# Dilated attention: queries and keys stored by residue, the scores of two heads issued in turn, weights read along the queries

## The chip, the cores and the metric

The kernel runs on one NeuronCore of a Trainium2 chip. A core has five engines with a queue each: TensorE (PE in the profile, with its weight loads listed apart as PEld), VectorE (DVE), ScalarE (ACT), GpSimd (POOL) and SyncE (SP, which only starts DMAs here). Matmuls read SBUF and write PSUM, which has 8 banks of 128 partitions by 512 floats. The metric is the time of one execution on the device in microseconds (us): 1367.67 us, the median of three runs before (1365.44 to 1367.97).

## The reference

A trunk of two layers over 512 tokens of width 1024, all in float32. Each layer is a mixer and a gated feed-forward, each between two normalizations with modulation. Layer 0's mixer is a pool and a gated recurrence; layer 1's is the dilated attention, the only part that the change touches:

```python
DIL_GROUPS = ((128, 1), (512, 4), (2048, 16))   # window, dilation; 8 heads of width 64 in each
def dilated_group_attention(q, k, v, win, dil, bias_table):
    blk = win // dil                              # 128 in all three groups
    qs = _to_strided(q * 64 ** -0.5, dil, blk)    # tokens regrouped by residue modulo dil
    kk, vv = with_prev(ks), with_prev(vs)         # a block sees itself and the one before it
    ...
    s = einsum(qs, kk) + bias;  s = where(mask, s, -inf)
    m = max(s);  p = exp(s - m);  l = sum(p)
    o = einsum(p, vv) / l
# the three groups are joined per head: o = sum(l * exp(m - max) * o) / sum(l * exp(m - max))
```

With 512 tokens, group 0 has four blocks of 128 (each query sees its own block and the one before), group 1 has four residues modulo 4 with one block of 128 tokens each, and group 2 (16 residues) is computed on the same four residues with a mask that leaves the tokens of the same residue modulo 16.

## The kernel before

The work is staged in time: mixer 0, feed-forward 0, attention (about 664 to 975 us of the profile), feed-forward 1. Activations lie feature by token. Weight matmuls use a split into two parts (`hi`, `lo`) and three products; they all go through the helper `mm`, so the profile puts them on L263. The attention's own score matmuls are plain float32 and stand on their own lines.

The order on each engine is found by a scheduler that replays the program with its own times when the program is built (`schedule_with_timeline_sim=True`). It may move an instruction ahead of another that it doesn't depend on; PSUM banks, though, are handed out where the code asks for them, from a queue: `bk.get()` takes the bank that was given back longest ago, `bk.free()` puts it at the end.

The function `attention` (L1220) runs as follows.

- The head (L1225 to L1237): the queries (even `i`, scaled by 0.125, on ACT, L1231) and keys (odd `i`, on DVE, L1233) of the first pair of heads are copied from PSUM into SBUF, `i` = 0 to 5 being q0, k0, q1, k1, q2, k2 of the three groups. A tile holds two heads, head `hh` on partitions 64*hh to 64*hh+63, with the 512 tokens along the row.
- `values` makes V for the three groups (L1273).
- Then four pairs of heads. For pairs 1 to 3, six projections of 24 matmuls each (L1289) with copies on ACT and DVE (L1293, L1295). For every residue `r` of 0 to 3 and each of the two heads: 7 score matmuls (L1320 to L1326) into one bank; a reduction on DVE that adds the bias and takes the maximum (L1333), which frees the bank; the exponential with its sum on ACT (L1338); reciprocal and scaling on DVE (L1340, L1341); four transposes on PE into a second bank (L1344); a copy of that bank to `PT` on ACT (L1346).
- `weighted` (L1352) multiplies `PT` by V: group 0 in four steps over key blocks with the queries of all residues at once (L1368 to L1370), groups 1 and 2 residue by residue (L1372).
- With pair 3, four of the eight banks are set aside for the output projection (L1300), `weighted` runs in two halves of the tokens, and the output projection's first matmuls may fill PE between the scores.

Of the 7 score matmuls of a head, five have weights of 64 rows by 32 columns: `far` (L1320, a constant that masks a block which doesn't exist) and group 0's quarter `j` = 0 (L1321) both stand in column group 0, quarters 1 to 3 (L1323) in column groups 1 to 3. The two others (L1326, groups 1 and 2) have weights of 64 rows by 128 columns. Head 0 uses rows 0 to 63 of the array and head 1 rows 64 to 127 (`tile_position`). The operands for residue `r` are read with a step of four floats: `qv[ps, j, :, r]`, `z.rearrange("p (i r) -> p r i")`-like views `[ps, :, r]` of q1, k1, q2, k2. Only k0 is read in the order of the tokens.

Of the kernel before, what the change touches and what calls it, by code (L numbers as in the profile page):

```python
# [15 lines left out]
AF = mybir.ActivationFunctionType  # L16
ALU = mybir.AluOpType

P = 128
# [3 lines left out]
HT = T // 2  # L23
# [157 lines left out]
def trunk(ctx: ExitStack, tc: tile.TileContext, a: dict, out: bass.AP, last: int = 3):  # L181
    nc = tc.nc
    pe, act, dve, pool, sp = nc.tensor, nc.scalar, nc.vector, nc.gpsimd, nc.sync
# [8 lines left out]
    ar, rr, tr = Arena(), Arena(), Arena()  # L192
# [8 lines left out]
    def swing_to(*arenas):  # L201

        first = next((i for i in range(2) if swings[i]["of"] is not arenas[i]), 2)
        for z in reversed(swings[first:]):
            if z["of"] is not None:
                for i in range(len(z["units"])):
                    z["of"].drop(f"{z['name']}{i}")
                z["pool"].__exit__(None, None, None)
            z["of"] = None
        for z, arena in list(zip(swings, arenas))[first:]:  # L210
            if arena is None:
                continue
            n_swing[0] += 1
            z["of"], z["pool"] = arena, tc.tile_pool(name=f"swing{n_swing[0]}", bufs=1, reuse_waits="tile")
            p = z["pool"].__enter__()
            for i, u in enumerate(z["units"]):
                name = f"{z['name']}{i}"
                t = p.tile([P, u * UNIT], F32 if arena is ar else F32R, tag=name, name=f"swing{n_swing[0]}_{i}")
                arena.add(name, t, u)
# [277 lines left out]
    b = bk.get()  # L497
# [401 lines left out]
    for h in range(4):  # L899
        b = banks8[4 + h]  # L900
# [319 lines left out]
    def attention(s, chain):  # L1220
        ahead.update(load=N_QK, split=N_QK - 1, f=8, r=0)
        head_banks = project_head(s, w_qk, N_QK, chain)
        rr.closed.discard("o")
        swing_to(ar, ar)
        head_rs = []  # L1225
        for i in range(N_QK):
            r = ar.get(1)
            for hf in range(2):
                o, y = ar.ap(r)[:, hf * HT : (hf + 1) * HT], bk[head_banks[hf][i // 2]][:, (i % 2) * HT : (i % 2 + 1) * HT]
                if i % 2 == 0:  # L1230
                    act.activation(o, y, AF.Copy, scale=0.125)  # L1231
                else:
                    dve.tensor_copy(o, y)  # L1233
            head_rs.append(r)
        for z in head_banks:
            for b in z:
# [40 lines left out]
        for pair in range(4):  # L1277
            qk_rs = []
            pt_rs = [ar.get(4) for _ in range(2)]
            for x in (pair, pair + 1):  # L1280
                if x < 4 and x not in biases_of:
                    load_biases(x)
            bias_r, bias_t = biases_of[pair]
            for i in range(6):
                if pair * 6 + i < N_QK:
                    qk_rs.append(head_rs[i])
                    continue
                b = bk.get()
                project(w_qk2 + pair * 6 + i - N_QK, b)  # L1289
                ada_step(44)  # L1290
                r = ar.get(1)
                if i % 2 == 0:
                    act.activation(ar.ap(r), bk[b], AF.Copy, scale=0.125)  # L1293
                else:
                    dve.tensor_copy(ar.ap(r), bk[b])  # L1295
                bk.free(b)
                qk_rs.append(r)
            if pair == 3:
                ahead.update(load=14, split=4, f=2, r=0)
                out_banks = [bk.get() for _ in range(4)]  # L1300
                rr.add("h", h_t, 2 * ND)
                rr.used["h"] = [k % ND < 4 for k in range(2 * ND)]
                for _ in range(2):
                    split_next(0, pool)
                for i, r in enumerate(o_rs):
                    split_into(h_hi[:, i, :], h_lo[:, i, :], ar.ap(r))
                    ar.free(r)
            q0, k0, q1, k1, q2, k2 = (ar.ap(r) for r in qk_rs)
            PT = [ar.ap(r).rearrange("p (r s q) -> p r s q", r=4, s=4) for r in pt_rs]
            for r in range(4):  # L1310
                for hh in range(2):
                    head = 2 * pair + hh
                    ps = slice(64 * hh, 64 * hh + 64)
                    b = bk.get()
                    qv = q0.rearrange("p (j i r) -> p j i r", j=4, r=4)
                    for j in range(4):
                        js = slice(32 * j, 32 * j + 32)
                        kw = dict(start=True, stop=True, tile_position=(64 * hh, 32 * j), skip_group_check=True)
                        if j == 0:
                            pe.matmul(bk[b][js, 0:P], far[ps, :], one_row[ps, :], **kw)  # L1320
                            pe.matmul(bk[b][js, P : 2 * P], qv[ps, j, :, r], k0[ps, 0:P], **kw)  # L1321
                        else:
                            pe.matmul(bk[b][js, 0 : 2 * P], qv[ps, j, :, r], k0[ps, (j - 1) * P : (j + 1) * P], **kw)  # L1323
                    for i, (q, k) in enumerate(((q1, k1), (q2, k2))):
                        qc, kc = (z.rearrange("p (i r) -> p i r", r=4)[ps, :, r] for z in (q, k))
                        pe.matmul(bk[b][:, (2 + i) * P : (3 + i) * P], qc, kc, start=True, stop=True, skip_group_check=True)  # L1326
                    sc_r = tr.get(1)
                    sc = tr.ap(sc_r)
                    two = lambda z: z.rearrange("p (s n) -> p s n", s=2)
                    base = bias_t[:, hh, 255 + r : 256 + r]  # L1330
                    bias = bass.AP(base.tensor, base.offset, [list(base.ap[0]), [W0 - r, 2], [-1, 256]])
                    m = col(1)
                    dve.tensor_tensor_reduce(  # L1333
                        out=two(sc), in0=two(bk[b]), in1=bias, scale=-1.0, scalar=3e38, op0=ALU.add, op1=ALU.min, accum_out=m
                    )
                    bk.free(b)
                    l = col(1)
                    act.activation(sc, sc, AF.Exp, bias=m, scale=-1.0, accum_out=l)  # L1338
                    rl = col(1)
                    dve.reciprocal(rl, l)  # L1340
                    dve.tensor_scalar(sc, sc, rl, None, ALU.mult)  # L1341
                    b = bk.get()
                    for i, seg in enumerate((1, 0, 2, 3)):
                        pe.transpose(bk[b][:, seg * P : (seg + 1) * P], sc[:, i * P : (i + 1) * P], ident)  # L1344
                    tr.free(sc_r)
                    act.activation(PT[hh][:, r, :, :], bk[b].rearrange("p (s q) -> p s q", s=4), AF.Copy)  # L1346
                    bk.free(b)
            for r in qk_rs:
                ar.free(r)
            ar.free(bias_r)  # L1350

            def weighted(b, first, end):  # L1352

                todo = []
                for kb in range(4):
                    js = [j for j in (kb, kb + 1) if first <= j < end]
                    if js:
                        todo.append((0, kb, js))
                for g in (1, 2):
                    for r in range(4):  # L1360
                        todo.append((g, r, None))
                for n, (g, x, js) in enumerate(todo):
                    for hh in range(2):
                        head = 2 * pair + hh
                        ps = slice(64 * hh, 64 * hh + 64)
                        if js:

                            base = PT[hh][:, 0, js[0] - x, 32 * js[0] : 32 * js[0] + 1]  # L1368
                            rhs = bass.AP(base.tensor, base.offset, [list(base.ap[0]), [160, len(js)], [1, 32], [512, 4]])
                            o = bk[b][ps, js[0] * P : (js[-1] + 1) * P]  # L1370
                        else:
                            rhs = PT[hh][:, x, 1 + g, 32 * first : 32 * end]  # L1372
                            o = bk[b][ps, :].rearrange("p (i r) -> p i r", r=4)[:, 32 * first : 32 * end, x]
                        lhsT = VV[g][:, x, head * 64 : head * 64 + 64]
                        mm(b if hh == 0 else (b, 1), o, lhsT, rhs, n == 0, n == len(todo) - 1)

            if pair < 3:
                b = bk.get()
                weighted(b, 0, 4)
                for r in pt_rs:  # L1380
                    ar.free(r)
                r = ar.get(1, "f")
                act.activation(ar.ap(r), bk[b], AF.Copy)
                bk.free(b)
                o_rs.append(r)
# [135 lines left out]
```

## Time and profile before

| what | value |
|---|---|
| median of 3 runs | 1367.67 us (1365.44 to 1367.97) |
| the profiled execution, its time | 1367.64 us |
| the profiled execution, its span (first to last instruction) | 1365.9 us |
| mean granted TensorE clock | 0.960 |
| PE busy | 1315.0 us (96%) |
| PEld busy | 1145.6 us (84%) |
| DVE busy | 651.9 us (48%) |
| ACT busy | 455.1 us (33%) |
| POOL busy | 271.3 us (20%) |

The span is what the trace holds; 1.74 us of the execution's time lie around it. A row of a group of instructions has the line, engine, operation, the tiles written and read, shapes and count, then busy time and mean duration. In a timeline a row is start, length, engine, line, tiles, shape and count of a run of like instructions. A row of the view by windows gives for a stretch its length, then each engine's busy time with its number of instructions, the granted TensorE clock, the DMA share and rate. The granted clock of TensorE takes two values in this trace, 1.0 and 0.5.

### The profile page before, as it was taken

What the parts mean: (1) busy time and instruction counts of PE and PEld (TensorE: products, weight loads), DVE (VectorE), ACT (ScalarE), POOL (GpSimd) and SP (SyncE); (2) the same over time, 40 slices, a digit from 0 to 9 for tenths busy, and PEclk for the clock granted to TensorE, in tenths of its full rate; (3) what the DMA queues carried; (4) which work ended last, traced back from release to release, by engine and by line L of the source; (5) the groups of instructions that cost most, each with busy time, mean ns of one, the idle gap of its engine ahead of it and who ended that gap; (6) DMA issues with size and microseconds to landing.
All of it is one profiled execution on the core that took longest, in us unless ns stands there. A gap on an engine that the chain in (4) does not pass through costs nothing.

```text
span 1365.9 us, 20678 instructions
## 1 busy us (share of the span) xinstructions
PE 1315.0 (96%) x8672; PEld 1145.6 (84%) x8672; DVE 651.9 (48%) x965; ACT 455.1 (33%) x743; POOL 271.3 (20%) x141
## 2 busy tenths in 40 slices
PE   8898798999999999999999999999899999999997
PEld 6676588998888899999897777777898888889997
DVE  6997866754443223448474032323766211223415
ACT  4341335632222222246324223333653222222303
POOL 4531622321111111313110002011221111111002
PEclk9999899999999999999997879898999999999999
DMA  7855333426552222413391103132135222222301
GB/s 271 320 168 176 124 124 124 139 100 221 187 185 77 77 93 93 155 52 119 128 316 51 47 24 115 47 124 93 47 124 201 92 77 85 85 77 94 109 1 62
DMA packets 50383, 164.25 MB, mean 120 GB/s; under 512 B 5809, under 2 KB 11081, under 8 KB 50290
## 3 DMA queue, kind: packets, MB, share of 16 engines
q1 hardware_dynamic: 50290, 162.93, 35.1%
q8 instruction: 68, 1.11, 0.3%
q14 instruction: 25, 0.20, 0.0%
HBM read 160.78 MB, written 2.13 MB: 119 GB/s over the span
## 4 chain that ended last, share of the span: by engine, by line
PE 83%; DVE 10%; ACT 2%; issue 2%; DMA 1%; POOL 1%; SPq 0%; DVEq 0%; ACTq 0%; POOLq 0%
PE bank L263 76%; DVE ada_w L403 3%; PE bank L1326 3%; PE bank L1344 1%; PE bank L1323 1%; PE bank L1320 1%; DVE swing L937 1%; DVE t L642 1%; DVE swing L284 1%; DVE r L284 0%; DVE swing L938 0%; PE bank L1321 0%; POOL cst L475 0%; DVE h L681 0%; DVE h L539 0%
## 5 line engine op out<-in xcount | busy, mean ns | idle before, releaser
L263 PE MATMUL bank<-h,r 128*128 128x512 f32 (+1 forms) x2104 | 471.0, 365 | 15.0 <-DVE f L927 7.6
L263 PEld LDWEIGHTS bank<-h,r 128*128 128x128 f32 x2104 | 366.9, 193 | 78.8 <-ACT h L522 8.4
L263 PE MATMUL bank<-h,swing 128*128 128x512 f32 (+1 forms) x1664 | 324.4, 342 | 5.0 <-ACT swing L351 2.2
L263 PEld LDWEIGHTS bank<-h,swing 128*128 128x128 f32 x1664 | 267.6, 190 | 41.4 <-DVE h L284 2.5
L284 POOL TENSOR_TENSOR r<-f,r 128x1024 fp32r<-128x1024 f32 x39 | 99.4, 2551 | 462.0 <-PE bank L263 282.0
L263 PE MATMUL bank<-o,swing 128*128 128x256 f32 x1280 | 158.9, 281 | 0.0
L263 PEld LDWEIGHTS bank<-o,swing 128*128 128x128 f32 x1280 | 154.1, 189 | 0.1
L351 ACT ACTIVATE r<-f 128x1024 fp32r<-128x1024 f32 x104 | 108.9, 1058 | 128.9 <-PE bank L263 97.9
L403 DVE SCALAR_TENSOR_TENSOR ada_w<-ada_w,sil 128x1025 f32<-128x1025 f32 x96 | 143.7, 1513 | 12.1 <-DMA ada_w<-ada 11.9
L284 DVE TENSOR_TENSOR r<-f,r 128x1024 fp32r<-128x1024 f32 (+1 forms) x51 | 69.5, 1364 | 160.5 <-PE bank L263 64.9
L284 POOL TENSOR_TENSOR swing<-f,swing 128x1024 fp32r<-128x1024 f32 x27 | 66.3, 2456 | 259.5 <-PE bank L263 219.2
L284 DVE TENSOR_TENSOR swing<-f,swing 128x1024 fp32r<-128x1024 f32 x45 | 59.9, 1336 | 121.2 <-PE bank L263 81.6
L351 ACT ACTIVATE swing<-f 128x1024 fp32r<-128x1024 f32 x80 | 83.5, 1057 | 86.0 <-PE bank L263 42.2
L263 PE MATMUL bank<-o,r 128*128 128x256 f32 x832 | 105.4, 281 | 0.0
L263 PEld LDWEIGHTS bank<-o,r 128*128 128x128 f32 x832 | 101.3, 189 | 0.1
L1193 ACT ACTIVATE t<-bank 128x512 f32<-128x512 f32 (+1 forms) x52 | 27.2, 531 | 175.3 <-PE bank L263 175.3
L263 PE MATMUL bank<-h,o 128*128 128x512 f32 (+1 forms) x312 | 81.7, 349 | 2.5 <-DVE h L681 1.7
L263 PE MATMUL bank<-r,h 128*128 128x512 f32 x288 | 70.9, 395 | 0.0
L263 PEld LDWEIGHTS bank<-r,h 128*128 128x128 f32 x288 | 61.8, 249 | 6.1 <-issue 0.4
L263 PEld LDWEIGHTS bank<-h,o 128*128 128x128 f32 x312 | 56.5, 193 | 10.4 <-DVE h L681 2.1
L475 POOL TENSOR_TENSOR cst<-cst 128x2 f32<-128x2 f32 (+1 forms) x19 | 17.8, 939 | 232.1 <-DVE cst L473 232.1
L284 DVE TENSOR_TENSOR o<-f,o 128x256 fp32r<-128x256 f32 (+2 forms) x37 | 24.6, 681 | 78.6 <-ACT o L565 74.4
(193 smaller groups left out, 1193.9 us busy)
## 6 DMA issues: line engine op xcount, KB each, us to landing
ada_w<-ada SPq DMA_DIRECT2D x96, 512.5 KB, 4.7
f<-w_fi SPq DMA_DIRECT2D x88, 512.0 KB, 4.5
f<-w_fo SPq DMA_DIRECT2D x44, 512.0 KB, 3.4
f<-w_aqk SPq DMA_DIRECT2D x24, 512.0 KB, 3.6
f<-w_av SPq DMA_DIRECT2D x12, 512.0 KB, 6.1
f<-w_qf SPq DMA_DIRECT2D x8, 512.0 KB, 5.0
f<-w_ho SPq DMA_DIRECT2D x8, 512.0 KB, 4.4
f<-x SPq DMA_DIRECT2D x8, 256.0 KB, 3.2
```

What stands on the lines that cost most here:

```text
L263: i = pe.matmul(o, lhsT, rhs, start=start, stop=stop, skip_group_check=True)
L284: eng.tensor_tensor(o, x, y, ALU.subtract)
L351: act.activation(hi, w, AF.Copy)
L403: dve.scalar_tensor_tensor(w, w, 1.0, sil, ALU.mult, ALU.mult, accum_out=mods[:, s, 2 * j + k : 2 * j + k + 1])
L475: pool.tensor_tensor(r, v, mhalf[:, 0:cols], ALU.pow)
L642: dve.tensor_tensor(us[i], us[i], rows, ALU.mult)
L937: dve.tensor_tensor(qv, qv, t_first.unsqueeze(2).broadcast_to([P, n, L]), ALU.mult)
L1193: act.activation(tr.ap(sa)[:, cols], a, AF.Silu)
L1320: pe.matmul(bk[b][js, 0:P], far[ps, :], one_row[ps, :], **kw)
L1323: pe.matmul(bk[b][js, 0 : 2 * P], qv[ps, j, :, r], k0[ps, (j - 1) * P : (j + 1) * P], **kw)
L1326: pe.matmul(bk[b][:, (2 + i) * P : (3 + i) * P], qc, kc, start=True, stop=True, skip_group_check=True)
L1344: pe.transpose(bk[b][:, seg * P : (seg + 1) * P], sc[:, i * P : (i + 1) * P], ident)
```

## The change

Four things change, all in `attention`.

1. `keep_qk` writes q0, q1, k1, q2 and k2 by residue: token 4*i + r goes to place 128*r + i, so that the copy reads PSUM with a step of four floats and writes runs. k0 stays in the order of the tokens. The head's copies (in halves of 256 tokens) and those of the projections both use it.
2. The score matmuls then read weights and moving operands of a residue as runs of neighbouring floats: 32 or 128 of them.
3. For each residue both heads' banks are taken first and the scores of the two heads are issued in turn, head 1 first, each tied behind the one before it by a dependency without a semaphore. In the code the reductions, exponentials and transposes of both heads follow after the scores of both.
4. In `weighted`, group 0's moving operand is read with the query index innermost (runs of 32 floats) and the residue outside, and the output view is turned to match, so that PSUM is written with a step of four floats.

```diff
+        def keep_qk(i, r, y, half=None):
+            o = ar.ap(r)
+            if i == 1:
+                o = o if half is None else o[:, half * HT : (half + 1) * HT]
+            else:
+                o = o.rearrange("p (r i) -> p r i", r=4)
+                o = o if half is None else o[:, :, half * HT // 4 : (half + 1) * HT // 4]
+                y = y.rearrange("p (i r) -> p r i", r=4)
+            if i % 2 == 0:
+                act.activation(o, y, AF.Copy, scale=0.125)
+            else:
+                dve.tensor_copy(o, y)
...
-                    act.activation(ar.ap(r), bk[b], AF.Copy, scale=0.125)
-                    dve.tensor_copy(ar.ap(r), bk[b])
+                keep_qk(i, r, bk[b])
...
+            halves_of = [slice(64 * hh, 64 * hh + 64) for hh in range(2)]
+            by_place = lambda z: z.rearrange("p (r i) -> p r i", r=4)
             for r in range(4):
+                banks2 = [bk.get() for _ in range(2)]
+                heads2 = list(enumerate(halves_of))[::-1]
+                before = [None]
+                def score(o, q, k, **kw):
+                    i = pe.matmul(o, q, k, start=True, stop=True, skip_group_check=True, **kw).ins
+                    if before[0]:
+                        tc.add_manual_dep(i, before[0], NOSYNC, reason="two heads at a time")
+                    before[0] = i.name
+                qv = q0.rearrange("p (r j i) -> p r j i", r=4, j=4)
+                for j in range(4):
+                    js = slice(32 * j, 32 * j + 32)
+                    for n in range(2 if j == 0 else 1):
+                        for hh, ps in heads2:
+                            kw = dict(tile_position=(64 * hh, 32 * j))
+                            o = bk[banks2[hh]]
+                            if j == 0 and n == 0:
+                                score(o[js, 0:P], far[ps, :], one_row[ps, :], **kw)
+                            elif j == 0:
+                                score(o[js, P : 2 * P], qv[ps, r, j, :], k0[ps, 0:P], **kw)
+                            else:
+                                score(o[js, 0 : 2 * P], qv[ps, r, j, :], k0[ps, (j - 1) * P : (j + 1) * P], **kw)
+                for i, (q, k) in enumerate(((q1, k1), (q2, k2))):
+                    for hh, ps in heads2:
+                        qc, kc = (by_place(z)[ps, r, :] for z in (q, k))
+                        o = bk[banks2[hh]][:, (2 + i) * P : (3 + i) * P]
+                        score(o, qc, kc)
                 for hh in range(2):
-                    b = bk.get()
+                    b = banks2[hh]
...
-    rhs = bass.AP(base.tensor, base.offset, [list(base.ap[0]), [160, len(js)], [1, 32], [512, 4]])
-    o = bk[b][ps, js[0] * P : (js[-1] + 1) * P]
+    rhs = bass.AP(base.tensor, base.offset, [list(base.ap[0]), [160, len(js)], [512, 4], [1, 32]])
+    o = bk[b][ps, js[0] * P : (js[-1] + 1) * P].rearrange("p (j i r) -> p j r i", j=len(js), r=4)
```

More of the change, by code (lines that the diff above doesn't have):

```diff
@@ L1228, in attention @@
             for hf in range(2):
[L1229 to L1233, printed above, removed]
+                keep_qk(i, r, bk[head_banks[hf][i // 2]][:, (i % 2) * HT : (i % 2 + 1) * HT], hf)
             head_rs.append(r)
@@ L1291, in attention @@
                 r = ar.get(1)
-                if i % 2 == 0:
-                    act.activation(ar.ap(r), bk[b], AF.Copy, scale=0.125)
-                else:
-                    dve.tensor_copy(ar.ap(r), bk[b])
+                keep_qk(i, r, bk[b])
                 bk.free(b)
@@ L1309, in attention @@
             PT = [ar.ap(r).rearrange("p (r s q) -> p r s q", r=4, s=4) for r in pt_rs]
+            halves_of = [slice(64 * hh, 64 * hh + 64) for hh in range(2)]
+            by_place = lambda z: z.rearrange("p (r i) -> p r i", r=4)
+            two = lambda z: z.rearrange("p (s n) -> p s n", s=2)
             for r in range(4):
-                for hh in range(2):
-                    head = 2 * pair + hh
-                    ps = slice(64 * hh, 64 * hh + 64)
-                    b = bk.get()
[L1315 to L1326, printed above, removed]
@@ L1327, in attention @@
+                for i, (q, k) in enumerate(((q1, k1), (q2, k2))):
[3 more added lines that the diff above has]
+                        score(o, qc, kc)
+                for hh in range(2):
+                    b = banks2[hh]
                     sc_r = tr.get(1)
                     sc = tr.ap(sc_r)
-                    two = lambda z: z.rearrange("p (s n) -> p s n", s=2)
```

## The prediction

> **What bounds the kernel now.** I read the page first: the span, the granted clock by slices, the chain that ended last. Then the view by windows for the four score stages (all engines, then L263 alone), and PE's timeline inside them.
>
> ```profile
> span 1365.9 us, 20678 instructions
> PEclk9999899999999999999997879898999999999999
> PE 83%; DVE 10%; ACT 2%; issue 2%; DMA 1%; POOL 1%; SPq 0%; DVEq 0%; ACTq 0%; POOLq 0%
> 728.48:763.53 35.05, 35.05 (x169) 23.62 (x168) 11.23 (x33) 13.30 (x26) 0.00 (x0) 0.61 0.08 17
> 797.70:820.62 22.92, 22.32 (x145) 16.13 (x145) 10.19 (x33) 8.89 (x22) 0.00 (x0) 0.63 0.15 41
> 859.54:887.20 27.66, 27.66 (x169) 20.56 (x169) 11.91 (x35) 10.74 (x24) 0.00 (x0) 0.75 0.16 58
> 920.64:954.93 34.29, 32.85 (x217) 25.88 (x217) 14.96 (x36) 10.96 (x25) 6.14 (x2) 0.85 0.26 93
> 728.48:763.53 35.05, 8.74 (x25) 5.63 (x24) 0.61 0.08 17
> 859.54:887.20 27.66, 8.03 (x27) 5.24 (x27) 0.75 0.16 58
> 920.64:954.93 34.29, 12.39 (x73) 10.62 (x73) 0.85 0.26 93
> 904.62 5.20 PE L263 MATMUL bank<-h,o 128*128 128x512 f32 x22
> 949.57 1.68 PE L263 MATMUL bank<-h 128*128 128x256 f32 x12
> ```
>
> The first three rows: PE carries 83% of the chain, and its clock dips in the attention. The next four are the score stages of the four pairs, from the first score to the last transpose: PE is busy nearly throughout, DVE and ACT 9 to 15 us each, the clock 0.61 to 0.85. So a stage is set by PE. Then come L263's matmuls inside: some 24 and 26 of the next pair's projections, at about 0.23 us each at full clock (22 in 5.2 us, the row after), and in pair 3 73 others, at 0.12 (12 in 1.5 us, the last row, until 951.09), 8.8 us. Net of the projections the stages cost 35.05 - 5.5 = 29.5, 22.9 and 27.66 - 6.0 = 21.7 us, together 74.1.
>
> Inside a stage, one head at full clock, and two at half clock:
>
> ```profile
> 728.48 0.29 PE L1320 MATMUL bank<-far 64*32 64x128 f32 x1
> 728.49 0.44 PE L1323 MATMUL bank<-swing 64*32 64x256 f32 x3
> 728.61 0.27 PE L1320 MATMUL bank<-far 64*32 64x128 f32 x1
> 728.72 0.27 PE L1321 MATMUL bank<-swing 64*32 64x128 f32 x1
> 728.76 0.39 PE L1323 MATMUL bank<-swing 64*32 64x256 f32 x3
> ...
> 729.08 1.29 PE L1326 MATMUL bank<-swing 64*128 64x128 f32 x4
> 730.30 0.29 PE L1320 MATMUL bank<-far 64*32 64x128 f32 x1
> 732.13 0.35 PE L1320 MATMUL bank<-far 64*32 64x128 f32 x1
> 734.39 0.42 PE L1320 MATMUL bank<-far 64*32 64x128 f32 x1
> ```
>
> L1320 shows two records for one call of a head: a float32 matmul is two passes. A head takes 730.30 - 728.48 = 1.82 us at full clock: 0.60 for the quarter-width part, where the three L1323 start together and the two passes of one column group follow each other by 0.11 (128 columns) or 0.27 us, and 1.22 for the four passes of L1326. At half clock it is 734.39 - 732.13 = 2.26.
>
> **The change part by part.** *Two heads in turn.* Do the halves of the rows run together? Three rows answer, from where the scheduler happened to put two heads' L1326 side by side:
>
> ```profile
> 802.76 0.61 PE L1326 MATMUL bank<-swing,f 64*128 64x128 f32 x2
> 802.76 1.30 PE L1326 MATMUL bank<-swing,f 64*128 64x128 f32 x6
> 803.99 0.42 PE L1321 MATMUL bank<-f 64*32 64x128 f32 x1
> ```
>
> The first row is a window of 0.03 us: two passes have begun. The second has six passes from 802.76 to 803.99, 1.23 us, where four took 1.22 above. Two passes lay beside two others. So I cost both heads' quarter part as one head's, 0.60 us per residue.
>
> The Trainium skill speaks against this: "TensorE: Matmul & The Clock Gate", Part 3, under "What overlaps and what doesn't", has matmuls start and end strictly in program order. By that rule each second pass would hold the other head back. The trace differs: L1323 starts at 728.49 and L1321, which the code issues before it, at 728.72.
>
> *Runs instead of steps of four.* L1326's passes follow each other by about 0.24 us, at either clock:
>
> ```profile
> L1326 PEld LDWEIGHTS bank<-swing x96: 304/327/329, 729.1 to 948.5; 64*128 64x128 f32 x96
> L263 PEld LDWEIGHTS bank<-cst,t 128*128 128x128 f32 x16 | 2.1, 190 | 1.9 <-ACT t L662 1.1 <-ACT t L633 0.8
> ```
>
> A load of 128 columns in steps takes 327 ns, one of 128 neighbouring floats 190 (the second row, sums of squares as weights). With runs I take a pass at the 0.11 us that L1320 shows for 128 neighbouring columns. Then the wide part is 0.19 for the first load, four passes of 0.11 in both halves of the rows at once, and 0.1 to drain: 0.75 us for two heads. A residue costs 0.60 + 0.75 = 1.35, say 1.4 us of PE instead of 3.6 (4.5 at half clock). Bounds: 0 saved by the runs (1.22 instead of 0.75) and 1.35.
>
> *What is late next.* A stage can't shrink to 4 x 1.4 us, because the work behind the scores stays:
>
> ```profile
> L1333 DVE CUSTOM_DVE_ANT_1 t<-bank,f x24: 685/692/693, 730.4 to 876.8; 128x512 f32<-128x512 f32 x24
> L1338 ACT ACTIVATE t<-t,cst x32: 705/722/727, 731.4 to 950.3; 128x512 f32<-128x512 f32 x32
> L1338 ACT ACTIVATION_READ_ACCUMULATOR t<-t,cst x32: 185/187/207, 732.1 to 951.0; 128x1 f32 x32
> L1340 DVE RECIPROCAL cst<-cst x32: 143/158/166, 732.9 to 951.2; 128x1 f32<-128x1 f32 x32
> L1341 DVE TENSOR_SCALAR t<-t,cst x32: 466/485/489, 733.1 to 951.4; 128x512 f32<-128x512 f32 x32
> 759.75 0.60 PE L1344 MATMUL bank<-cst,t 128*128 128x128 f32 x4
> 760.11 0.71 PE L263 MATMUL bank<-h,r 128*128 128x512 f32 x2
> L1346 ACT ACTIVATE swing<-bank x28: 578/597/641, 741.0 to 954.9; 128x512 f32<-128x512 f32 x28
> ```
>
> One head behind its scores: 0.69 + 0.72 + 0.19 + 0.16 + 0.49 + 0.36 (transposes, 759.75 to 760.11) + 0.60 = 3.2 us, with six hand-overs of about 0.1 some 4.0. ACT needs 0.72 + 0.19 + 0.60 = 1.5 us a head, 12 us a stage, and becomes the pace.
>
> And the banks tie it: a residue now takes two banks at once from the ring. Counting through eight banks, residues 0 and 1 find theirs free; residue 2's second bank is that of the transposes of residue 0's first head, residue 3's that of residue 1's first head. Head 1 is issued first and all is tied in order, so a waiting head stops both. Pairs 0 to 2 at full clock: scores of residues 0 and 1 until 2.8 us; residue 2 starts after 1.4 + 0.1 + 4.0 = 5.6 and ends at 7.0; residue 3 starts near 8.0 (two more ACT turns) and ends at 9.4. Projections of the next pair then fill PE: the first bank they can have is residue 2's second score bank, free at 7.0 + 2 x 0.8 = 8.6. Behind 9.4 lie five heads' transposes, 5 x 0.46 with changes of shape: 11.7. I add 0.5 for the wait on k2's copy, which other heads' scores used to cover, and 0.8 for windows at half clock that remain: **13 us a stage**, 39 instead of 74.1, so **-35**. The transposes' return to full clock is in it.
>
> Pair 3 has four banks. There each residue's scores wait for the transposes of the residue before, a period of 1.4 + 0.1 + 4.0 = 5.6 with rounding. k2 comes as late as now:
>
> ```profile
> 925.22 0.88 PE bank L1326 x4
> L1295 DVE COPY swing<-bank x5: 676/691/692, 797.8 to 924.5; 128x512 f32<-128x512 f32 x5
> ```
>
> From residue 0's end at 925.8 three periods lead to 942, then 1.4 + 4.0 + 1.5 (the second head on ACT) to 949 instead of 954.93: **-5**, with 1 us left for half clock. The 8.8 us of L263 fit the gaps.
>
> *Weights read along the queries.* Group 0 of `weighted`, then groups 1 and 2, at full clock:
>
> ```profile
> 893.60 0.61 PE L263 MATMUL bank<-f,swing 128*64 128x256 f32 x1
> 894.03 0.61 PE L263 MATMUL bank<-f,swing 128*64 128x256 f32 x1
> ...
> 896.62 0.27 PE L263 MATMUL bank<-f,swing 128*64 128x128 f32 x1
> ...
> 896.73 0.27 PE L263 MATMUL bank<-f,swing 128*64 128x128 f32 x1
> ```
>
> A pass of 256 columns read 2 KB apart takes 0.43 us, one of 128 neighbouring columns 0.11, and that one already writes PSUM in steps of four. So a pass of 256 falls to 0.22. A pair has three calls of 256 and one of 128, two passes each, both heads side by side: 6 x 0.21 + 2 x 0.11 = 1.5 us; four pairs **-6**. Bounds 0 and -6.
>
> *The copies.* 25 copies now read PSUM in steps; no row shows that. From below nothing, from above double (0.69 us more, the length of L1295): ACT and DVE are free at that time, and only k2's copy stands before a score, 4 x 0.7 = 3 us. I take 0, since L1333 reads PSUM at the same 0.69 us with other steps in its second operand. The cover is the next projection on PE, 24 matmuls, 5.5 us.
>
> Sum: -35 - 5 - 6 = **-46 us** on the span, and on the median: 1367.67 - 46 = **1321.5 us** (the profiled execution took 1367.64).
>
> **The rivals.**
>
> *The stage stays long* (18%): the scheduler puts transposes ahead of projections in PE's queue, and PE waits while the clock stays at half, as it did for the score windows above. For it: pair 1's stage ran without a projection inside. Then a residue's period of about 4.2 us is not filled: 17 a stage, nothing in pair 3, -23 - 6: 1339.
>
> *Strict order between the heads* (6%): each second pass blocks. Per residue 4 x 0.11 + 6 x 0.22 + 0.3 for the quarter part and 0.8 for the wide one, 2.8 us instead of 1.4. Against it: the 728.49 and 802.76 rows. Four of these with transposes fill 15 us, with waits and half clock again 17 a stage: 1339. The Trainium skill's rule named above would give this.
>
> *PE filled throughout* (12%): the waits of residues 2 and 3 are covered. Then a stage is 4 x 1.4 + 8 x 0.46 = 9.3 us, -46, pair 3 -9, weights -6: 1306.
>
> *The turn between residues becomes the bound* (4%, slower): if PE's queue holds all transposes of a residue ahead of the next residue's scores, and no projection between, every residue costs the whole chain: scores, reduction, exponential, scaling, and the second head's transposes one ACT turn later. At full clock that is 1.4 + 0.1 + 3.4 + 1.5 = 6.4 us, at half clock about 1.4 more (scores and transposes), 7.8. Now a residue costs (74.1 + 34.3 - 8.8)/16 = 6.2, with the weights' gain 6.6: from there on it is slower, at 7.8 by 16 x 1.2 = 19 us: 1387. Against it: banks of residue 1 are free at once, and the scheduler mixes shapes now.
>
> *Nothing comes of it* (2%): DVE and ACT were the pace all along, and PE's shorter scores turn into waits: 1367. PE's full rows, with DVE and ACT at a third to a half, speak against it.
>
> **How the numbers follow.** Forecast 58%, its own range 1307 to 1336. The range for 8 in 10 takes in most of the longer stages and half of the filled ones: 1305 to 1346. A measurement of this kernel can tell about 0.2% from no change. Faster 0.94 (the first four cases), same 0.02, slower 0.04.
>
> **What would show it.** Right: the two heads' matmuls starting together, as the three L1323 do now; a wide weight load near 190 ns; about 1.4 us per residue; the 256-column passes of `weighted` 0.22 apart; the score windows' clock above 0.8; PE waiting for ACT's copy of `PT` before residues 2 and 3. Wrong: the wide passes still 0.24 apart, the second head's passes behind the first's, or PE idle for more than 4 us in a stage.

## The result and the profile after

The changed kernel takes 1334.1 us (median of four runs, 1328.02 to 1337.58) beside 1366.56 for the kernel before on the same chip: ratio 0.9758, 95% interval 0.9727 to 0.9789. That is 32 us less, where 46 were forecast. A second set of five runs on another occasion gave 1335.26 (ratio 0.9763, 0.9739 to 0.9786). The profiled execution took 1336.7 us with a span of 1334.9.

From the page of the changed kernel, its span, the granted clock by slices, and the engines' shares of the chain that ended last:

```profile
span 1334.9 us, 20663 instructions
PEclk9997899999999999999999899987999999999999
PE 80%; DVE 13%; ACT 3%; issue 2%; DMA 2%; POOL 1%; SPq 0%; DVEq 0%; ACTq 0%; POOLq 0%
```

PE's share of the chain fell from 83% to 80%, and DVE's rose from 10% to 13%: PE now waits more. The view by windows for the four score stages of the changed kernel, first all engines (PE, PEld, DVE, ACT, POOL, clock, DMA share, GB/s), then L263 alone in the first three:

```profile
731.37:760.22 28.85, 26.09 (x197) 19.82 (x196) 11.75 (x34) 12.86 (x27) 1.41 (x1) 0.82 0.07 15
785.23:805.60 20.37, 15.91 (x163) 12.02 (x163) 10.18 (x33) 11.02 (x24) 1.68 (x1) 0.92 0.19 48
838.76:857.72 18.96, 15.94 (x166) 12.33 (x165) 10.12 (x34) 9.37 (x22) 0.00 (x0) 0.91 0.17 57
888.89:923.50 34.61, 23.46 (x217) 19.49 (x216) 14.98 (x36) 11.08 (x24) 6.14 (x2) 0.76 0.28 92
731.37:760.22 28.85, 13.53 (x53) 10.36 (x52) 0.82 0.07 15
785.23:805.60 20.37, 4.47 (x19) 3.33 (x19) 0.92 0.19 48
838.76:857.72 18.96, 6.09 (x26) 4.36 (x25) 0.91 0.17 57
```

Before, PE was busy nearly throughout a stage; now it is idle for 3 to 11 us of each. Less 52, 18 and 25 projections at 0.23 us, the first three stages cost 16.9 + 16.2 + 13.2 = 46.3 us, where 74.1 were paid before and 39 forecast. Pair 3's stage takes 34.61 us; it took 34.29 before, and 5 less were forecast.

PE's timeline in the changed kernel shows the first stage (start, length, engine, line, tiles, shapes, count; in brackets the idle time before it and what ended it):

```profile
731.37 0.30 PE L1329 MATMUL bank<-far 64*32 64x128 f32 x2
731.40 0.43 PE L1329 MATMUL bank<-swing 64*32 64x256 f32 x6
731.51 0.28 PE L1329 MATMUL bank<-far 64*32 64x128 f32 x2
731.62 1.08 PE L1329 MATMUL bank<-swing 64*32 64x128 f32 x18
732.62 0.30 PE L1329 MATMUL bank<-far 64*32 64x128 f32 x2
...
735.92 1.04 PE L1370 MATMUL bank<-cst,t 128*128 128x128 f32 x4 [1.98 <-DVE t L1367]
737.74 1.97 PE L1370 MATMUL bank<-cst,t 128*128 128x128 f32 x8 [0.78 <-DVE t L1367]
739.64 0.42 PE L1329 MATMUL bank<-far 64*32 64x128 f32 x2
```

Both heads' first matmuls stand in one row, x2, and six quarter-width ones in the next: the two halves of the rows work together. From 731.37 to 732.62 both heads' scores of a residue take 1.25 us. Then PE has nothing: residues 0 and 1 are done at 733.9, the transposes come when DVE has scaled `sc` (L1367), and residue 2 begins at 739.64, 8.3 us into the stage.

Where the time went, over the whole attention (before 668.48 to 1000.61, after 671.37 to 969.17; the other kernels likewise: each stretch begins 60 us ahead of the first score matmul and ends, to about 0.5 us, at the same point behind the output projection). The time from each matmul's start to the next one's is put down to the first, less the part that lies behind the ends of all matmuls, which is idle. "Half clock" is the length of the stretches in which 0.5 was granted.

| kernel | attention | scores | transposes | `weighted` | PE idle | half clock |
|---|---|---|---|---|---|---|
| before | 332.1 | 73.4 | 18.3 | 23.2 | 5.7 | 68.3 |
| changed | 297.8 | 25.6 | 22.6 | 15.3 | 25.9 | 37.5 |
| e1: banks by role | 277.4 | 28.2 | 15.3 | 14.0 | 10.3 | 6.8 |
| e4: two in turn alone | 311.4 | 33.8 | 23.3 | 21.7 | 23.3 | 41.0 |
| e5: all but the turn | 313.9 | 61.0 | 18.1 | 15.8 | 6.6 | 58.0 |
| e6: no tie | 291.3 | 33.9 | 15.8 | 16.3 | 13.9 | 10.2 |
| e7: one bank per head | 272.2 | 24.7 | 15.1 | 14.0 | 10.6 | 3.4 |
| e10: e5 with one bank per head | 304.6 | 56.3 | 19.0 | 15.6 | 4.5 | 47.8 |

PE's work fell by 47.8 us on scores and 7.9 on `weighted`. Of these, 20.2 came back as idle time and 4.3 as slower transposes, which the change doesn't touch; PE's other matmuls took some 3 us less. The attention is 34.3 us shorter and the span 31.0: the changed kernel's first score matmul comes 2.9 us later, and by the same count the profiled executions of all kernels here begin the attention anywhere from 666.2 to 672.1. What lies ahead of it is the same code, so this is a difference between executions and not the change's work.

### The profile page after: what moved, and what is told of

It reads as the page before. It is cut to its first block, busy times and chain, and to the rows that moved or that the text cites. A ratio compares the mean times of both kernels' runs of the same rounds, so it can differ in the third digit from the quotient of the medians.

```text
span 1334.9 us, 20663 instructions
## 1 busy us (share of the span) xinstructions
PE 1265.7 (95%) x8672; PEld 1117.5 (84%) x8672; DVE 654.2 (49%) x965; ACT 455.3 (34%) x743; POOL 270.3 (20%) x141
## 4 chain that ended last, share of the span: by engine, by line
PE 80%; DVE 13%; ACT 3%; issue 2%; DMA 2%; POOL 1%; SPq 0%; DVEq 0%; ACTq 0%; POOLq 0%
PE bank L263 76%; DVE ada_w L403 3%; PE bank L1370 1%; PE bank L1329 1%; DVE swing L937 1%; DVE t L1359 1%; DVE r L284 1%; DVE swing L938 1%; DVE swing L284 1%; DVE t L642 1%; ACT t L1364 0%; DVE h L681 0%; DVE f L646 0%; DVE h L539 0%; DMA f<-w_ho 0%
## 5 line engine op out<-in xcount | busy, mean ns | idle before, releaser
L263 PE MATMUL bank<-h,r 128*128 128x512 f32 (+1 forms) x2104 | 470.1, 365 | 15.7 <-DVE f L927 7.9
L263 PEld LDWEIGHTS bank<-h,r 128*128 128x128 f32 x2104 | 367.0, 193 | 79.6 <-ACT h L522 8.7
L263 PE MATMUL bank<-h,swing 128*128 128x512 f32 (+1 forms) x1664 | 325.0, 343 | 3.5 <-ACT swing L351 2.2
L263 PEld LDWEIGHTS bank<-h,swing 128*128 128x128 f32 x1664 | 268.1, 191 | 39.9 <-ACT swing L351 2.4
L263 PE MATMUL bank<-o,swing 128*128 128x256 f32 x1280 | 159.2, 281 | 0.0
L263 PEld LDWEIGHTS bank<-o,swing 128*128 128x128 f32 x1280 | 154.2, 189 | 0.1
L284 DVE TENSOR_TENSOR r<-f,r 128x1024 fp32r<-128x1024 f32 (+1 forms) x51 | 73.8, 1448 | 161.3 <-PE bank L263 64.0
L263 PE MATMUL bank<-o,r 128*128 128x256 f32 x832 | 105.4, 281 | 0.0
L263 PEld LDWEIGHTS bank<-o,r 128*128 128x128 f32 x832 | 101.3, 189 | 0.1
L263 PE MATMUL bank<-h,o 128*128 128x512 f32 (+1 forms) x312 | 81.6, 347 | 2.5 <-DVE h L681 1.7
L263 PE MATMUL bank<-r,h 128*128 128x512 f32 x288 | 70.9, 395 | 0.0
L263 PEld LDWEIGHTS bank<-r,h 128*128 128x128 f32 x288 | 61.8, 249 | 6.1 <-issue 0.4
L263 PEld LDWEIGHTS bank<-h,o 128*128 128x128 f32 x312 | 56.0, 192 | 10.6 <-DVE h L681 2.1
```

The source lines that it names most:

```text
L263: i = pe.matmul(o, lhsT, rhs, start=start, stop=stop, skip_group_check=True)
L284: eng.tensor_tensor(o, x, y, ALU.subtract)
```

## The experiments

Twelve runs were made, the last of them the changed kernel again. e1 to e4 were timed against 1367.04 us for the kernel before, e5 to e8 against 1366.68, e9 and e10 against 1365.70, e11 and e12 against 1366.61. Each expectation names its theories; in e1, e6, e7 and e11 the first is about PE's new idle time as a wait for banks in a ring.

**e1, banks by role.** A residue takes four banks at once, two for scores and two for transposes, and gives all back at its end.

```diff
                 banks2 = [bk.get() for _ in range(2)]
+                banks_t = [bk.get() for _ in range(2)]
...
-                    bk.free(b)
                     l = col(1)
...
-                    b = bk.get()
+                    b = banks_t[hh]
...
-                    bk.free(b)
+                for b in (*banks2, *banks_t):
+                    bk.free(b)
```

> The changed kernel with one difference: a residue takes its two score banks and its two transpose banks together and gives all four back at its end, so a score bank is always an old score bank, which the reduction frees, and no residue waits for the copy of the transposes (L1372) of an earlier one. Theory 1, the banks' ring holds the next residue back: PE's idle time in the score stages (2.8, 4.5, 3.0 and 11.8 us in the changed kernel) falls to about half, and the time from 1334 to about 1324, most of it in pair 3's stage (34.6 us to about 28). Theory 2, the work on ACT and DVE behind the scores and the half clock set the pace, whatever the banks: within 3 us of the changed kernel, the idle time only moves.

Measured: 1312.13 us, ratio 0.9594 (0.9575 to 0.9613), 22 us less than the changed kernel and twice what theory 1 gave. The waits of PE over the attention that bear on this, first in the changed kernel and then in e1 (what waited, for what: total us, times, longest):

```profile
PE bank L1370 <- DVE t L1367: 17.4, 9, 3.0
PE bank L1329 <- DVE swing L1238: 2.3, 1, 2.3
...
PE bank L1329 <- ACT swing L1372: 1.4, 2, 0.7
```

```profile
PE bank L1330 <- DVE swing L1238: 2.3, 1, 2.3
PE bank L1330 <- DVE cst L1360: 1.8, 4, 0.8
...
PE bank L1370 <- DVE t L1367: 0.9, 2, 0.5
```

In the ring, the bank that residue 2's scores need is one into which transposes went, so they wait for the whole chain, and PE stands in front of the next transposes (L1370) with nothing to do. With roles a score bank is free as soon as DVE has reduced it (L1360), and the scores of residues 2 and 3 fill that time. The 17.4 us fall to 0.9.

**e2, runs alone.** The kernel before with `keep_qk` and operands read by residue, in the old order of the heads.

```diff
-                    qv = q0.rearrange("p (j i r) -> p j i r", j=4, r=4)
+                    qv = q0.rearrange("p (r j i) -> p r j i", r=4, j=4)
...
-                        qc, kc = (z.rearrange("p (i r) -> p i r", r=4)[ps, :, r] for z in (q, k))
+                        qc, kc = (z.rearrange("p (r i) -> p r i", r=4)[ps, r, :] for z in (q, k))
```

> The kernel before with operands by residue alone (part 1 and 2 of the change), the heads one after the other as before, the weights read as before. A head's passes of L1326 fall from 0.24 us to 0.11 at full clock or 0.21 at half clock, a head from 1.82 to about 1.25 us or from 2.26 to about 1.95. Theory 1, the stages before were set by PE: 32 heads save 10 (half clock) to 18 us (full), 1349 to 1357. Theory 2, the work behind the scores was the pace already: under 4 us, 1363 or more.

Measured: 1350.3 us, ratio 0.9881 (0.9862 to 0.9900), 17 less than before, as theory 1 has it: the stages before were set by PE. The scores fell from 73.4 to 54.4 us of PE.

**e3, `weighted` alone.** The kernel before with the fourth part of the change.

```diff
-[list(base.ap[0]), [160, len(js)], [1, 32], [512, 4]]
+[list(base.ap[0]), [160, len(js)], [512, 4], [1, 32]]
-o = bk[b][ps, js[0] * P : (js[-1] + 1) * P]
+o = bk[b][ps, js[0] * P : (js[-1] + 1) * P].rearrange("p (j i r) -> p j r i", j=len(js), r=4)
```

> The kernel before with the weights read along the queries alone (part 4). The passes of 256 columns go from 0.43 to 0.22 us; the four weighted stages take 23.2 us before and 15.3 in the changed kernel: -6 to -8 us, 1359 to 1361, nothing else moves. If PE had waited behind them for something else: under 3 us.

Measured: 1362.12 us, ratio 0.9963 (0.9946 to 0.9980), 5 less, with an interval of 2.7 to 7.4. That is short of the 6 to 8 expected, though the interval reaches into them. `weighted` did fall as expected, from 23.2 to 15.8 us of PE; the profiled execution has 75.1 us at half clock in the attention instead of 68.3.

**e4, two heads in turn alone.** The changed kernel with queries and keys in the order of the tokens and `weighted` read as before.

```diff
-            if i == 1:
+            if True:
...
-            by_place = lambda z: z.rearrange("p (r i) -> p r i", r=4)
+            by_place = lambda z: z.rearrange("p (i r) -> p r i", r=4)
```

> The changed kernel with queries and keys in the order of the tokens and the weights read as before: the two heads in turn alone (part 3). A residue takes 0.60 + 1.22 = 1.8 us of PE at full clock instead of 3.6, 0.5 more than in the changed kernel. If the residues' turns (banks and the chain behind the scores) set the pace of the changed kernel's stages, most of those 16 x 0.5 us hide in PE's idle time, and the time is that of the changed kernel plus the weights' 8 us and 2 to 4 more: 1344 to 1347. If PE sets the pace there too: 8 + 8 more, 1350 or over.

Measured: 1348.86 us, ratio 0.9856 (0.9835 to 0.9878), 18 less, between the two theories. From here to the changed kernel, 8.2 us of scores and 6.4 of `weighted` go, PE's idle time rises by 2.6, and the median falls by 14.8: what the scores shed is not hidden. Scores that stand in series with their residue's chain would give this; no run tries it by itself.

**e5, all but the turn.** e2 and e3 together.

> The change without its third part: queries and keys by residue and weights read along the queries, but one head behind the other as before. Theory 1 (the parts on TensorE simply add, and the turn's own gain is what PE's waits eat): 1350.3 - 4.9 = 1345 us, 1342 to 1348, so that the turn is worth 11 us in the changed kernel, against 18 alone. Theory 2 (the turn gains its full 18 us beside the others): 1334 + 18 = 1352, 1350 to 1355.

Measured: 1344.13 us, ratio 0.9827 (0.9800 to 0.9854): theory 1. Alone the turn is worth 18 us (e4), beside the other parts only 10, while PE's time on scores falls by 35.4 from e5 to the changed kernel.

**e6, without the tie.** The changed kernel without `tc.add_manual_dep`.

```diff
-                    if before[0]:
-                        tc.add_manual_dep(i, before[0], NOSYNC, reason="two heads at a time")
```

> The changed kernel without the dependency that ties the heads' scores to one another. Theory 1 (the ring of banks alone makes residue 2 wait, in whatever order the scheduler puts the heads): within 4 us of 1334. Theory 2 (the tie is what stops a head whose bank is free behind one whose bank is not): 1320 to 1328, with less PE idle in the stages, as with the four banks per residue.

Measured: 1327.45 us, ratio 0.9716 (0.9702 to 0.9731), some 7 less than the changed kernel, with intervals that just touch (up to 0.9731 here, from 0.9727 there). The time lies at the upper end of theory 2's range, and the idle time halves, as theory 2 has it; but in residue 2 the scheduler then runs the heads one behind the other, and scores cost 33.9 us instead of 25.6. The tie is a loss, then, but the smaller one: e1 gives 22 us with the tie in place.

**e7, one bank per head.** A head's transposes go into the bank of its own scores, which is given back behind the copy to `PT`.

```diff
-                    bk.free(b)
                     l = col(1)
...
-                    b = bk.get()
                     for i, seg in enumerate((1, 0, 2, 3)):
```

> The changed kernel, with each head's transposes written into the bank of its own scores, which is given back only behind the copy to PT: two banks per residue, so eight banks hold four residues and pair 3's four banks hold two. Theory 1 (the wait for another residue's bank is the loss): no residue of pairs 0 to 2 waits for another, 16 us a stage as with separate roles, and pair 3 falls from 28 to some 24, as two residues are under way at once: 1308 us, 1304 to 1312. Theory 2 (what counts is that banks come free early for the next pair's projections; here the first is free 4 us later than in the changed kernel): PE idles there instead, 1318 to 1328.

Measured: 1305.31 us, ratio 0.9557 (0.9542 to 0.9572): theory 1, and the fastest version here with e8, 61 us below the kernel before and 29 below the changed one. The four stages in the view by windows of e7, then L263 alone in the first three:

```profile
726.25:741.00 14.75, 13.89 (x165) 10.79 (x165) 10.48 (x33) 12.53 (x28) 0.00 (x0) 1.00 0.09 20
773.24:789.06 15.82, 15.26 (x168) 11.71 (x168) 9.70 (x33) 9.99 (x24) 2.39 (x1) 1.00 0.26 68
821.76:837.88 16.12, 14.24 (x161) 11.01 (x161) 10.55 (x34) 10.07 (x24) 0.00 (x0) 1.00 0.28 100
869.56:892.84 23.28, 20.46 (x217) 16.83 (x216) 14.37 (x36) 10.82 (x25) 6.14 (x2) 0.93 0.38 136
...
726.25:741.00 14.75, 5.83 (x21) 3.41 (x21) 1.00 0.09 20
773.24:789.06 15.82, 5.49 (x24) 4.17 (x24) 1.00 0.26 68
821.76:837.88 16.12, 5.49 (x23) 3.99 (x23) 1.00 0.28 100
```

PE is idle 0.6 to 1.9 us in each of the first three, the clock stays at 1.00, and less 20, 23 and 22 projections they cost 10.2 + 10.5 + 11.1 us. Pair 3 falls from 34.61 to 23.28, for with two residues under way its four banks are enough.

**e8, k2 on ACT.** As e7, with k2's copy on ACT.

```diff
                 act.activation(o, y, AF.Copy, scale=0.125)
+            elif i == 5:
+                act.activation(o, y, AF.Copy)
             else:
```

> As e7_same_bank, with the copies of k2 on ACT instead of DVE. Theory 1 (in pair 3 k2's copy stands behind DVE's long L284 rows and PE waits 2.3 us for it, and nothing covers that): 2 us less than e7_same_bank. Theory 2 (with two residues under way the scores of the next cover it, or ACT, with twelve us of work a stage, hands the wait on): within 1 us of it.

Measured: 1305.72 us, ratio 0.9556 (0.9536 to 0.9577), no change against e7. PE's timeline in pair 3, in e7 and then in e8:

```profile
874.14 0.66 PE L1329 MATMUL bank<-swing 64*128 64x128 f32 x4 [2.33 <-DVE swing L1238]
```

```profile
875.01 0.49 PE L1331 MATMUL bank<-swing 64*128 64x128 f32 x4
...
879.33 1.11 PE L1370 MATMUL bank<-cst,t 128*128 128x128 f32 x4 [2.57 <-DVE t L1368]
```

The wait for k2 is gone, and one of the same length stands in front of the first transposes: the wait was handed on.

**e9 and e10, one bank per head without the turn.** The edit of e7 in the kernel before (e9) and in e5 (e10).

> The kernel before with one edit: the transposes go into the bank of their head's own scores. Theory 1 (the banks tie nothing before the change: PE waits 5.7 us in the whole attention there, since a head takes one bank at a time and its slow scores cover the chain of the other): within 4 us of 1367. Theory 2 (the roles of the banks are a loss of their own, apart from the change): 1335 to 1350.

> e5_no_turn (all but the heads in turn) with the same edit. Theory 1 (without the turn PE's own scores are the bound and the banks are not): within 5 us of 1344, so that with the banks out of the way the turn is worth 1344 - 1305, near 39 us, where it is worth 10 in the changed kernel. Theory 2 (shorter scores already wait for banks): 1325 to 1335.

Measured: e9 1364.52 us, ratio 0.9982 (0.9963 to 1.0001); e10 1340.35, ratio 0.9799 (0.9757 to 0.9841). Theory 1 in both: banks are no loss until the turn makes PE's part short. With banks out of the way the turn is worth 1340.35 - 1305.31 = 35 us, give or take 6 by e10's interval, and in the changed kernel 10.

**e11, the other head's chain first; e12, the changed kernel again.** In the changed kernel head 1's scores are issued first, and the scheduler runs its chain first too, but banks are handed out in the order of the code, head 0 first. The order of PE's queue, which is that of the built program and not a view of the profile, shows which bank residue 2 then needs:

```
L1370 MATMUL bank_70<-cst,t 128x128 x4
L1370 MATMUL bank_73<-cst,t 128x128 x4
L1370 MATMUL bank_75<-cst,t 128x128 x4
L1329 MATMUL bank_73<-far
L1329 MATMUL bank_72<-far
```

Bank 73 is that of the second chain. ACT's timeline in the changed kernel has the copies out of banks 70 and 73:

```profile
737.23 0.58 ACT L1372 ACTIVATE swing<-bank 128x512 f32<-128x512 f32 x1
...
738.89 0.60 ACT L1372 ACTIVATE swing<-bank 128x512 f32<-128x512 f32 x1 [0.38 <-PE bank L1370]
```

Residue 2 began at 739.64, behind the second. e11 turns the loop round:

```diff
-                for hh in range(2):
+                for hh in (1, 0):
                     b = banks2[hh]
```

> The changed kernel with the loop over the two heads' reductions, exponentials and transposes turned round, head 1 first, as its scores are. Banks are handed out in the order of the code, so residue 2 then needs the bank of the chain that runs first, and not that of the second. Theory 1 (that is the part of the wait that the forecast's 5.6 us left out: residue 2 began 8.3 us after the stage did, 0.15 us behind the second copy to PT and 1.8 us behind the first): residue 2 begins some 1.5 us sooner, 1 to 2 us a stage and 1 to 1.5 us for each of pair 3's three turns: 5 to 9 us less than the changed kernel. Theory 2 (any bank of transposes in the ring costs the same, as PE's queue holds the transposes in front of the scores anyway): within 3 us of the changed kernel.

> The changed kernel once more, beside e11_chain_order on the same chip: 1334 us, 1330 to 1338.

Measured: e11 1334.55 us (ratio 0.9762, 0.9738 to 0.9785), e12 1335.26 (0.9763, 0.9739 to 0.9786), as expected: no difference between the two, so theory 2. PE's timeline in e11:

```profile
732.11 0.30 PE L1329 MATMUL bank<-far 64*32 64x128 f32 x2
...
738.48 0.66 PE L1370 MATMUL bank<-cst,t 128*128 128x128 f32 x4 [1.16 <-DVE t L1367]
739.07 0.30 PE L1329 MATMUL bank<-far 64*32 64x128 f32 x2
```

Residue 2 does come 1.3 us sooner, 7.0 us into the stage, but PE is idle for the same 25.9 us over the attention. Which bank of transposes residue 2 needs makes no difference; e1 and e7, where it needs none in pairs 0 to 2, take 22 and 29 us less.

## Why the prediction was right, and where it was too large

**The sign and PE's own part were right, and the time lies in the range; the saving was forecast 14 us too large.** The time lies 2 us inside the upper end of the forecast's own range (1307 to 1336), so little more would have put it outside. By its terms on the span: 46 forecast, less 7.3 in pairs 0 to 2 (46.3 us instead of 39), less 5.3 in pair 3 (0.3 longer instead of 5 shorter), plus 1.9 in `weighted`, less 3.3 outside the attention, gives 32; 31.0 were measured, and the last 1.0 is not explained.

**PE's own part: right.** Groups of the changed kernel (busy, mean ns | idle before): the wide weight loads of pair 1 and the copies from PSUM in steps, both over the score stages, and `weighted`'s passes of 256 over the attention; below them the last group in the kernel before.

```profile
L1329 PEld LDWEIGHTS bank<-swing,f 64*128 64x128 f32 x16 | 1.2, 187 | 0.2 <-issue 0.2
L1238 DVE COPY swing<-bank 128x512 f32<-128x512 f32 x5 | 3.4, 689 | 18.2 <-PE bank L263 18.2
L263 PE MATMUL bank<-swing,swing 128*64 128x256 f32 x38 | 6.3, 415 | 0.7 <-ACT swing L1372 0.7
```

```profile
L263 PE MATMUL bank<-swing,swing 128*64 128x256 f32 x38 | 12.8, 636 | 0.0
```

A wide load takes 187 ns (190 forecast, 327 before); of all 128 in the changed kernel, the 104 that began at full clock took 182 to 188 ns and the 24 at half clock 260 to 334. The copies in steps take the same 0.69 us as before, so the term that was put at nothing was right, and the 256-wide passes half of what they did. A residue costs 1.25 us, where 1.35 to 1.4 was forecast. By the Trainium skill's rule of strict program order ("TensorE: Matmul & The Clock Gate", Part 3, "What overlaps and what doesn't") it would be the 2.8 us that the prediction worked out; the trace disagrees with the rule for matmuls in different halves of the rows.

**The wait of residue 2: seen, but mis-sized.** The step "residue 2 starts after 1.4 + 0.1 + 4.0 = 5.6" gave 8.3 in pair 0, 8.9 in pair 1 and 8.6 in pair 2. In pair 0 the bank was the right one, that of head 0's transposes, but head 0's chain ran second, and ACT had 1.28 us of table load to do in the first one. What the order of the chains cost is small by e11. In pairs 1 and 2 the transposes of all four heads before it, 16 matmuls, ran ahead of residue 2's scores, and PE waited in front of them for DVE. The prediction has it wait for ACT's copy to `PT`; that wait is seen in pair 3 alone, twice 0.7 us. PE's timeline in pair 1:

```profile
790.54 3.61 PE L1370 MATMUL bank<-cst,t 128*128 128x128 f32 x16 [2.01 <-DVE t L1367]
794.08 0.30 PE L1329 MATMUL bank<-far 64*32 64x128 f32 x2
```

The larger error in these pairs is the term of "0.8 for windows at half clock that remain". Two stretches of the changed kernel in the view by windows, one of pair 0 and one of pair 3:

```profile
736.10:746.30 10.20, 9.42 (x50) 6.88 (x50) 5.37 (x18) 5.31 (x12) 0.00 (x0) 0.50 0.01 2
...
893.10:899.90 6.80, 4.07 (x20) 3.78 (x21) 2.93 (x9) 2.12 (x5) 1.93 (x1) 0.50 0.54 189
```

In pairs 0 to 2 stretches at half clock make up 10.2 + 3.4 + 3.4 = 17 us, each of them following on a wait of 2 to 3 us. The transposes there cost 16.2 us, against 11.0 by the forecast's 8 x 0.46 a stage; that alone is 5.2 of the 7.3 us. The scores cost 18.6 us, against 16.8 by its 4 x 1.4, and the projections 1.2 more than their 0.23 us each. The idle time, 10.2 us in the three, was 1.5 above the 8.8 that its waits leave (2.8 + 1.0 + 0.5 a stage, less three transposes of 0.46). Less the 2.4 set aside for half clock, these make up the 7.3.

**Pair 3: the step "the 8.8 us of L263 fit the gaps" failed.** PE's timeline of the changed kernel there:

```profile
893.48 0.80 PE L1329 MATMUL bank<-swing 64*128 64x128 f32 x4 [2.33 <-DVE swing L1238]
896.63 1.11 PE L1370 MATMUL bank<-cst,t 128*128 128x128 f32 x4 [2.36 <-DVE t L1367]
897.39 3.75 PE L263 MATMUL bank<-h 128*128 128x256 f32 x20
900.98 0.60 PE L1370 MATMUL bank<-cst,t 128*128 128x128 f32 x4
901.33 2.63 PE L263 MATMUL bank<-h 128*128 128x256 f32 x20
...
904.61 0.30 PE L1329 MATMUL bank<-far 64*32 64x128 f32 x2
...
910.43 0.30 PE L1329 MATMUL bank<-far 64*32 64x128 f32 x2 [0.69 <-ACT swing L1372]
...
914.23 1.97 PE L1370 MATMUL bank<-cst,t 128*128 128x128 f32 x8 [2.47 <-DVE t L1367]
```

The output projection's matmuls stand in a row in front of residue 1's scores, which begin at 904.61, 10.3 us behind residue 0's end at 894.28, where the forecast gave 5.6 - 1.4 = 4.2. For the gaps behind residues 2 and 3, of 2.5 us each, none were left. The periods after that, 5.8 and 6.5 us, were near the 5.6 forecast.

**The rivals.** The result lies between the forecast and "the stage stays long" (1339), and nearer to the latter. Its mechanism is seen too: pairs 0 and 1 cost 16.9 and 16.2 us, where it has 17 and the forecast 13 (pair 2, with 13.2, is the forecast's); pair 3 gained nothing, as there; and PE waited in front of transposes, with half clock behind. Two of the signs that the prediction named went against it: PE was idle for over 4 us in pairs 1 and 3 (4.5 and 11.2), and pair 3's clock was 0.76, not above 0.8. "PE filled throughout" (1306) needed the waits of residues 2 and 3 covered; e7, which covers them, takes 1305.31. That agreement is in part luck: e7's stages cost 10.2 to 11.1 us and not 9.3, and pair 3 and `weighted` save 11.0 and 9.2 instead of 9 and 6. That the lost gain is those waits and the half clock behind them is shown by e1 and e7; how much of it is the clock alone was not tried.

## What to carry to other kernels

When one engine's part of a chain becomes short, ask what fills the chain's latency now: here the turn took 35 us of scores off PE, and 25 of them came to nothing until the next residues' scores could start without the last one's transposes. Buffers drawn from one ring in the order of the code tie a quick user to a slow one; give them roles, or let a chain keep its own buffer to the end. And price an idle stretch of PE with the slow clock behind it, not by its length alone.

## What the runs showed of the hardware

- **Half clock follows on short waits.** In the changed kernel each wait of PE of 1.98 us or more in the four stages was followed or accompanied by a stretch at half clock, 3.4, 6.8, 10.2 or 13.7 us long, whole multiples of 3.4. In e7 a wait of 1.64 us brought none and one of 2.33 brought 3.4 us. This gives no threshold, for e4's first stage fell to half clock for 10.2 us (from 734.83) right behind a wait of 0.75 us. The Trainium skill ("TensorE: Matmul & The Clock Gate", "Why this matters for your kernels") asks for no gaps of PE above about 3 us; here half clock followed on shorter ones, of 2 us and less.
- **PE drops to half clock without any wait.** The first stage of e10, whose heads run one behind the other:

```profile
731.65:761.48 29.83, 29.83 (x165) 19.77 (x165) 11.12 (x33) 13.08 (x26) 0.00 (x0) 0.66 0.06 14
```

PE is busy for all of its 29.83 us, at a clock of 0.66. The same stage of e7, which differs from e10 in the turn alone, has idle time and a clock of 1.00. So with one bank per head the turn saves twice: it uses both halves of the rows at once, and the clock stays up. What lowers it in e10 is not shown. In e10's pair 3 (907.70 to 930.27), where the heads also run one behind the other but the output projection's matmuls of 128 rows stand between, the clock is 1.00; the unused half of the rows as the cause would fit both stages, but no run tries it by itself.
